# A pooling mixer in front of a gated ConvFFN: zero tile, rows spread by TensorE, whole weights for two tiles, and the second norm turned in transpose mode

## The chip, the cores and the metric

The kernel runs on one core of a Trainium2 chip. The metric is the device time of one execution in microseconds, median of the runs shown. PE is TensorE, DVE VectorE, ACT ScalarE, POOL GpSimd, and SP the queue that issues all transfers of this kernel.

## The reference

One layer on x of 1024 tokens by 1024 columns, float32:

```python
h = rms_norm(x, norm_mix_g)
# pool_mixer: four column groups, causal windows of 2, 4, 8 and 16 tokens
d[g] = window_sum(h[g], w_len) / count - h[g]
y = scale * (einsum('bsgc,gcd->bsgd', d, w) + b)      # w: four 256x256 blocks
x = x + y
f = rms_norm(x, norm_ffn_g)
h = causal_depthwise_conv(f @ w_in, conv_w, conv_b)   # w_in: 1024 x 5632
val, gate = split(h)
out = x + (silu(gate) * val) @ w_out                  # w_out: 2816 x 1024
```

## The kernel before

All products are in float32 accuracy. A large product splits each operand into a high part (float32r, made by a copy on ACT) and the rest (a subtraction on DVE), and adds three products of these. The two ConvFFN products are done in seven block products of halves (a Strassen scheme: P1 to P7), for which sums and differences of blocks are made by DVE. They make up most of the time.

The change is in what comes before: the mixer and the making of the first product's right operand. The tokens lie in eight tiles of 128 (j = 0 to 7). One loop over j, unrolled, has these steps, each some rounds behind the one before:

- `stat(j)` calls `rstd_of` (L127): ACT squares the tile with a row sum, takes a root, and DVE gets the reciprocal and makes it more exact by a Newton step, five [128, 1] operations in all.
- `mixer_norm(j)` (L145): DVE multiplies the window matrix `band` by this, per token.
- `mixer_window(j)` (L188): eight f32 matmuls (`windows`, L149) turn the tile and apply windows and norm (`psd`). The first 16 tokens of a tile also need the tile before: `edges` holds this, made at once for all tiles from `x_edge`, the last 16 rows of each tile (`edge_norm`, `mixer_edges`). Then ACT and DVE split psd into `dh` and `dl`.
- `mixer_weights` and `mixer_bias` (L175, L157), once: DVE scales the mixer's weights by both gains, ACT and DVE split them into `wph` and `wpl`; the bias comes from rows read 128 times over.
- `mixer_out(j)` (L206): 24 matmuls of 256 columns and two of 512 for the bias (`psy`), the residual add on DVE (L217), a store of x1, the second norm's statistic, and DVE scales an identity by it (`diag`).
- `ffn_operand(j)` (L233): eight f32 matmuls with `diag` as the moving operand turn x1 and norm it (`pst`). ACT multiplies seven column blocks by the gain, DVE the eighth (`n2f`). Then come the splits of blocks B11 and B21 for tiles 0 to 3, and for tiles 4 to 7 differences of blocks and their splits.

Matmuls are shown in the trace as one record for float32r and bf16, two for float32. An engine works through its instructions in order. The order is set when the program is built, by a planner that takes what is ready by its own estimates of times, earlier code first; `tc.issue_after(ins)` puts the instructions of a block behind `ins` on the same engine. SP issues transfers in order and waits in order. Tiles of one tag share their buffers; a new one waits until the one before in its place is released. `x0`, `x1` and `x7` lie in the tag "hl", where later the split operands lie. `wp_raw` and `rows_b` lie in the tag "raw", into which `load_in` later loads blocks of w_in.

## Time and profile before

| | |
|---|---|
| median of 3 runs | 721.17 us (720.72 to 721.32) |
| profiled execution, its own time | 723.45 us |
| span of its profile | 721.7 us |
| TensorE busy, instructions | 698.9 us (97%), x3252 |
| VectorE busy | 609.7 us (84%), x941 |
| ScalarE busy | 352.3 us (49%), x566 |
| GpSimd busy | 7.7 us (1%), x33 |
| DMA | 83.83 MB, mean 116 GB/s |

The profile is of one execution. Its span is a little shorter than that execution's time, which also holds what lies before the first and behind the last instruction. Busy times of matmuls overlap, since matmuls are pipelined: the spacing of their starts, which the chain of work gives, is what one costs in a row of them. The same holds for VectorE and ScalarE, where an instruction can start some 0.07 us before the one ahead of it ends.

### The profile page before, as it was taken

To read this page: it belongs to the slowest core of one execution; us is meant where nothing else is said; L and a number is where in the kernel's file an instruction comes from. 1 tells how busy PE (TensorE), PEld (TensorE's weight loads), DVE (VectorE), ACT (ScalarE), POOL (GpSimd) and SP (SyncE) were. 2 spreads that over 40 slices of the span, in tenths; PEclk is the share of its full clock that TensorE was granted. 3 is DMA by queue.
4 is the path that set the end of the run, shared out by engine and by line. 5 is a ranking of instruction groups with operands and counts; after the bars stand their busy time and mean duration, and the time that the engine had idled before them with its cause. 6 is when DMAs were issued, how large, how long until landed. Compare 5 with 4: busy or idle time off the path is not lost.

```text
span 721.7 us, 8803 instructions
## 1 busy us (share of the span) xinstructions
PE 698.9 (97%) x3252; PEld 580.2 (80%) x3252; DVE 609.7 (84%) x941; ACT 352.3 (49%) x566; POOL 7.7 (1%) x33
## 2 busy tenths in 40 slices
...
DMA packets 30881, 83.83 MB, mean 116 GB/s; under 512 B 3335, under 2 KB 4487, under 8 KB 28023
## 3 DMA queue, kind: packets, MB, share of 16 engines
...
## 4 chain that ended last, share of the span: by engine, by line
PE 80%; DVE 11%; DMA 6%; issue 1%; SPq 1%; ACT 1%; DVEq 0%; ACTq 0%
PE Y L303 23%; PE oP L576 21%; PE X L303 15%; PE Z L303 15%; PE psy L214 3%; DMA blk<-g_dram 3%; PE psd L151 2%; DMA x<-in_x_dram 1%; PE pst L237 1%; DVE n2f L271 1%; DVE oBP L70 1%; DVE T L260 1%; DMA blk<-in_w_out_dram 1%; DVE blk L271 1%; DVE oAP L70 1%
## 5 line engine op out<-in xcount | busy, mean ns | idle before, releaser
L576 PE MATMUL oP<-oBP,oAP 128*128 128x512 f32 x924 | 210.8, 390 | 1.0 <-ACT oBP L69 0.6
L576 PEld LDWEIGHTS oP<-oBP,oAP 128*128 128x128 f32 x924 | 173.2, 188 | 38.5 <-DVE oBP L70 1.4
L303 PE MATMUL X<-B,A11s 128*128 128x512 f32 x264 | 65.6, 394 | 0.7 <-DVE A11s L70 0.7
L303 PE MATMUL Y<-T,S2s 128*128 128x512 f32 x264 | 65.1, 394 | 1.1 <-DVE T L260 1.0
L303 PE MATMUL Z<-B,S4s 128*128 128x512 f32 x264 | 64.1, 392 | 0.6 <-DVE r L337 0.6
L303 PE MATMUL Z<-T,S1s 128*128 128x512 f32 x264 | 64.6, 393 | 0.0
L303 PE MATMUL Y<-T,S3s 128*128 128x512 f32 x264 | 64.3, 392 | 0.0
L303 PE MATMUL Y<-T,A22s 128*128 128x512 f32 x264 | 64.1, 392 | 0.0
L303 PE MATMUL X<-B,A12s 128*128 128x512 f32 x264 | 63.4, 390 | 0.0
L303 PEld LDWEIGHTS Y<-T,S2s 128*128 128x128 f32 x264 | 49.2, 188 | 13.2 <-DVE T L260 1.5
L303 PEld LDWEIGHTS X<-B,A11s 128*128 128x128 f32 x264 | 49.3, 188 | 12.3 <-DVE A11s L70 1.1
L303 PEld LDWEIGHTS Z<-B,S4s 128*128 128x128 f32 x264 | 49.5, 188 | 11.8 <-issue 1.1
L303 PEld LDWEIGHTS Z<-T,S1s 128*128 128x128 f32 x264 | 49.5, 188 | 11.4 <-ACT S1s L69 0.2
L303 PEld LDWEIGHTS Y<-T,S3s 128*128 128x128 f32 x264 | 49.6, 188 | 11.2
L303 PEld LDWEIGHTS Y<-T,A22s 128*128 128x128 f32 x264 | 49.5, 188 | 11.1 <-ACT val L350 0.3
L303 PEld LDWEIGHTS X<-B,A12s 128*128 128x128 f32 x264 | 49.5, 188 | 10.3
L361 ACT ACTIVATE gate<-gate 128x1024 f32<-128x1024 f32 x22 | 23.4, 1061 | 43.5 <-DVE gate L352 43.5
L69 ACT ACTIVATE oBP<-blk 128x512 fp32r<-128x512 f32 x32 | 20.2, 633 | 46.9 <-PE oP L576 41.6
L351 DVE SCALAR_TENSOR_TENSOR val<-ha,par_sb,val 128x1023 f32<-128x1023 f32 x22 | 28.2, 1282 | 12.5 <-ACT val L350 12.5
L343 DVE TENSOR_TENSOR ha<-Z,q 128x512 f32<-128x512 f32 x20 | 13.8, 691 | 23.9 <-PE Z L303 23.9
L69 ACT ACTIVATE S4s<-win 128x512 fp32r<-128x512 f32 x22 | 13.9, 633 | 40.4 <-PE Z L303 35.9
L350 ACT ACTIVATE gate<-hb,par_sb 128x1024 f32<-128x1024 f32 x22 | 27.4, 1245 | 11.9 <-DVE hb L345 11.9
(130 smaller groups left out, 1094.2 us busy)
## 6 DMA issues: line engine op xcount, KB each, us to landing
...
g_dram<-val SPq DMA_DIRECT2D x22, 512.0 KB, 2.6
...
x<-in_x_dram SPq DMA_DIRECT2D x8, 512.0 KB, 10.4
x_dram<-x SPq DMA_DIRECT2D x8, 512.0 KB, 2.6
```

The lines of the kernel that those rows point to most:

```text
L69: nc.scalar.activation(t[:, 0, :], src, AF.Copy)
L70: nc.vector.tensor_tensor(t[:, 1, :], src, t[:, 0, :].bitcast(F32), ALU.subtract)
L151: nc.tensor.matmul(ps[:, c * P : (c + 1) * P], src[:, c * P : (c + 1) * P], weights[:, c // 2, :], start=True, stop=True)
L214: nc.tensor.matmul(o, a[:, c, :], w[:, c, :], start=c % 4 == 0 and i == 0, stop=False, skip_group_check=True)
L237: nc.tensor.matmul(ps[:, c * P : (c + 1) * P], x1[:, c * P : (c + 1) * P], diag, start=True, stop=True)
L271: nc.vector.tensor_tensor(out, a, b, ALU.subtract)
L303: nc.tensor.matmul(bank, a[:, i, ks], b[:, l, k, :], start=opens and m == 0, stop=m == 11, skip_group_check=not opens)
L343: tt(hid[n, "a"][:, NH:], bank, hid[n, "q2"], ALU.add)
L350: nc.scalar.activation(t, src, AF.Identity, bias=par_sb[:, CB + f : CB + f + 1], scale=w[2])
L351: nc.vector.scalar_tensor_tensor(t[:, 1:], src[:, : S - 1], w[1], t[:, 1:], op0=ALU.mult, op1=ALU.add)
L361: nc.scalar.activation(gate, gate, AF.Silu)
L576: nc.tensor.matmul(obanks[set_, i], a[:, u, i * P : (i + 1) * P], b[:, v, :], start=opens and g == 0 and m == 0, stop=g == NP2 - 1 and m = ...
```

## The change

- The first transfers are the scale row (on one partition) and both rows as 8 x 128 blocks, then x0, the constants (the first tile's windows now in bf16), the parameters and the weights, x1, x_edge, two rows of the bias, and x2 to x7. The broadcast reads of scale and bias are gone.
- TensorE starts with eight matmuls on a tile of zeros, and runs six more behind the first windows (`keep_warm`). Two matmuls with ones spread the scale row over the partitions, into PSUM, where `mixer_weights` reads it.
- The bias is multiplied and split on 8 partitions and goes by DMA into two rows of a tile that GpSimd has zeroed.
- The norm has three small operations in place of five: the scale by the number of columns is folded into constants (`FOLD`), and root and reciprocal are multiplied in by the instruction that uses them.
- Tiles 0 and 1 are not split: eight f32 matmuls of 256 columns with `wp_raw` take the place of 24. The split of the weights is a step of its own behind the edges' norm.
- The second norm is applied by DVE before the turn: `ffn_norm` multiplies x1 by the statistic and by the gain, which `gain_rows` has spread over the partitions. `ffn_operand` then turns it by `nc.tensor.transpose`, and the splits read PSUM; `n2f` is filled by one ACT copy (half of one for tiles 4 to 7).
- The input sums of the first two hidden blocks are made in rounds 9 and 10 of the loop (`sums_in`).

The diff, cut:

```diff
+FOLD = 2 * D**0.5
...
 NOPS_A = 3
-ACT_GAIN = 7
+XBUFS = 4
+WHOLE = 2
...
     def load_x(j):
-        if j < 2 or j == NS - 1:
+        if j < 2 or j >= 2 + XBUFS:
             xs[j] = work.tile([P, D], F32, tag="hl", name=f"x{j}", bufs=7)
         else:
-            xs[j] = pp.tile([P, D], F32, tag="x", name=f"x{j}", bufs=5)
+            xs[j] = pp.tile([P, D], F32, tag="x", name=f"x{j}", bufs=XBUFS)
...
     wp_raw = raw_tile("wp_raw").rearrange("p a (c d) -> p (a c) d", d=GRP)
-    rows_b = raw_tile("rows_b")
-    scale_b, bias_b = rows_b[:, 0, :], rows_b[:, 1, :]
+    rows_raw = raw_tile("rows_raw")
+    row_sb = rows_raw[:1, 0, :]
+    rows8, bias8 = (rows_raw[:NK, 1, i * NH : i * NH + 2 * P].rearrange("k (r p) -> k r p", p=P) for i in range(2))
+    bias8 = bias8.bitcast(F32R)
+    idle = work.tile([P, NH], BF16, tag="sum", name="idle", bufs=3)
+    nc.vector.memset(idle, 0.0)
+    idle_ps = bank2("idle_ps")[:, :NH]
+    def keep_warm(n):
+        for _ in range(n):
+            nc.tensor.matmul(idle_ps, idle[:, :P], idle, start=True, stop=True)
+    keep_warm(8)
+    nc.sync.dma_start(row_sb, rows[:1, :])
+    nc.sync.dma_start(rows8, rows.rearrange("r (k p) -> k r p", p=P))
     load_x(0)
     nc.sync.dma_start(cst, consts)
-    nc.sync.dma_start(x_edge[HALO:, :], x.rearrange("(j r) d -> j r d", r=P)[: NS - 1, P - HALO :, :])
     nc.sync.dma_start(par_sb, par)
-    nc.sync.dma_start(scale_b, rows[:1, :].to_broadcast([P, D]))
-    load_x(1)
     for g in range(0, NG, 2):
         nc.sync.dma_start(wp_raw[:, 2 * g : 2 * g + 4, :], pool_w[g : g + 2].rearrange("g (k p) d -> p (g k) d", p=P))
-    load_x(2)
-    nc.sync.dma_start(bias_b, rows[1:, :].to_broadcast([P, D]))
-    for j in range(3, NS):
+    b8 = rows8[:, 1, :]
+    nc.vector.tensor_tensor(b8, b8, rows8[:, 0, :], ALU.mult)
+    nc.scalar.activation(bias8[:, 0, :], b8, AF.Copy)
+    nc.vector.tensor_tensor(bias8[:, 1, :], b8, bias8[:, 0, :].bitcast(F32), ALU.subtract)
+    load_x(1)
+    nc.sync.dma_start(x_edge[HALO:, :], x.rearrange("(j r) d -> j r d", r=P)[: NS - 1, P - HALO :, :])
+    spread = work.tile([P, NK, P], F32, tag="hl", name="spread", bufs=7)
+    bias_hl = work.tile([P, D], F32R, tag="hl", name="bias_hl", bufs=7)
+    nc.gpsimd.memset(bias_hl.bitcast(F32), 0.0)
+    for l in range(2):
+        nc.sync.dma_start(bias_hl[l : l + 1, :].bitcast(F32), bias8[:, l, :].bitcast(F32))
+    for j in range(2, NS):
         load_x(j)
     eps_t = const.tile([P, 1], F32, tag="eps", name="eps_t")
-    nc.vector.memset(eps_t, EPS)
+    nc.vector.memset(eps_t, D * EPS)
+    warm = pp.tile([P, 1], F32, tag="warm", name="warm")
+    nc.scalar.activation(warm, eps_t, AF.Sqrt)
     ident = cst[:, :FAC]
     fac = cst[:, FAC:B0].rearrange("p (c t) -> p c t", t=HALO)
-    band0 = cst[:, B0:].rearrange("p (g s) -> p g s", s=P)
+    band0 = cst[:, B0:].bitcast(BF16).rearrange("p (g s) -> p g s", s=P)
...
         nc.scalar.activation(junk, src, AF.Square, accum_out=st[:, 0:1])
...
+        marks[name] = nc.scalar.activation(st[:, 1:2], st[:, 0:1], AF.Sqrt, bias=eps_t).ins
+        nc.vector.tensor_scalar(st[:, 0:1], st[:, 0:1], D * EPS, None, op0=ALU.add)
+        nc.vector.scalar_tensor_tensor(st[:, 3:4], st[:, 1:2], st[:, 1:2], st[:, 0:1], op0=ALU.mult, op1=ALU.add)
+        nc.vector.reciprocal(st[:, 2:3], st[:, 3:4])
+        return st[:, 1:2], st[:, 2:3]
+    def normed(out, src, r):
+        return nc.vector.tensor_scalar(out, src, r[0], r[1], op0=ALU.mult, op1=ALU.mult).ins
+    bands, stats = {}, {}
     def edge_norm():
-        nc.vector.tensor_scalar(edge_band, edge_band, rstd_of(x_edge, "e"), None, op0=ALU.mult)
+        marks["edge"] = normed(edge_band, edge_band, rstd_of(x_edge, "e"))
     def mixer_norm(j):
         t = bands[j] = pp.tile([P, NG, P], F32, tag="bandr", name=f"bandr{j}", bufs=2)
-        nc.vector.tensor_scalar(t, band if j else band0, stats[j], None, op0=ALU.mult)
+        marks[f"band{j}"] = normed(t, band if j else band0, stats[j])
...
+    ones = pp.tile([P, P], F32R, tag="ones", name="ones")
+    nc.vector.memset(ones.bitcast(F32), 1.0)
+    scale_b = []
+    for h in range(2):
+        t = ps_x.tile([P, NH], F32, tag="X", name=f"scale{h}")
+        nc.tensor.matmul(t, ones[:1, :].bitcast(F32), row_sb[:, h * NH : (h + 1) * NH], start=True, stop=True)
+        scale_b += [t[:, :GRP], t[:, GRP:]]
...
     def mixer_weights():
         for c in range(2 * NG):
-            g = c // 2
             nc.vector.scalar_tensor_tensor(
-                wp_raw[:, c, :], scale_b[:, g * GRP : (g + 1) * GRP], par_sb[:, GM + c : GM + c + 1], wp_raw[:, c, :], op0=ALU.mult, op1=ALU.mult
+                wp_raw[:, c, :], scale_b[c // 2], par_sb[:, GM + c : GM + c + 1], wp_raw[:, c, :], op0=ALU.mult, op1=ALU.mult
             )
...
-    ds = {}
+    def split_weights():
+        for c in range(0, 2 * NG, 2):
+            cs = slice(c, c + 2)
+            nc.scalar.activation(wph[:, cs, :], wp_raw[:, cs, :], AF.Copy)
+            nc.vector.tensor_tensor(wpl[:, cs, :], wp_raw[:, cs, :], wph[:, cs, :].bitcast(F32), ALU.subtract)
+    def gain_rows():
+        gain = par_sb[:, GF : GF + NK].unsqueeze(2).to_broadcast([P, NK, P])
+        nc.vector.tensor_tensor(spread, ident[:, None, :].to_broadcast([P, NK, P]), gain, ALU.mult)
+        ps = bank2("ps_gain")
+        flat = spread.rearrange("p k s -> p (k s)")
+        for h in range(2):
+            cols = slice(h * NH, (h + 1) * NH)
+            nc.tensor.matmul(ps[:, cols], ones.bitcast(F32), flat[:, cols], start=True, stop=True)
+        gain_b = work.tile([P, D], F32, tag="ha", name="gain_b", bufs=1)
+        nc.scalar.activation(gain_b, ps, AF.Copy, scale=FOLD)
+        return gain_b
+    ds, gains = {}, []
     def mixer_window(j):
         ps = bank2(f"psd{j}")
-        windows(ps, xs[j], bands.pop(j))
+        last = windows(ps, xs[j], bands.pop(j))
+        if j == 0:
+            with tc.issue_after(last):
+                keep_warm(6)
+        if j == 1:
+            mixer_edges()
         dh = pp.tile([P, NK, P], F32R, tag="dh", name=f"dh{j}", bufs=2)
-        dl = pp.tile([P, NK, P], F32R, tag="dl", name=f"dl{j}", bufs=1)
         ps3 = ps.rearrange("p (c s) -> p c s", c=NK)
         first = ps3[:, :, :HALO]
         if j == 0:
-            nc.vector.tensor_tensor(first, first, fac, ALU.mult)
+            marks["first"] = nc.vector.tensor_tensor(first, first, fac, ALU.mult).ins
         else:
             nc.vector.tensor_tensor(first, first, edges[:, :, j * HALO : (j + 1) * HALO], ALU.add)
+        if j < WHOLE:
+            dh = dh.bitcast(F32)
+            marks[f"whole{j}"] = nc.scalar.activation(dh, ps3, AF.Copy).ins
+            ds[j] = [(dh, wp_raw)]
+            return
+        dl = pp.tile([P, NK, P], F32R, tag="dl", name=f"dl{j}", bufs=1)
         nc.scalar.activation(dh, ps3, AF.Copy)
         nc.vector.tensor_tensor(dl, ps3, dh.bitcast(F32), ALU.subtract)
-        ds[j] = (dh, dl)
+        ds[j] = [(dh, wph), (dh, wpl), (dl, wph)]
...
-        dh, dl = ds.pop(j)
+        terms = ds.pop(j)
         ps = bank2(f"psy{j}")
+        for c in range(NK):
+            o = ps[:, c // 2 * GRP : (c // 2 + 1) * GRP]
+            for i, (a, w) in enumerate(terms):
+                nc.tensor.matmul(o, a[:, c, :], w[:, c, :], start=c % 4 == 0 and i == 0, stop=False, skip_group_check=True)
         for h in range(2):
             cols = slice(h * NH, (h + 1) * NH)
-            for c in range(4 * h, 4 * h + 4):
-                o = ps[:, c // 2 * GRP : (c // 2 + 1) * GRP]
-                for i, (a, w) in enumerate(((dh, wph), (dh, wpl), (dl, wph))):
-                    nc.tensor.matmul(o, a[:, c, :], w[:, c, :], start=c % 4 == 0 and i == 0, stop=False, skip_group_check=True)
-            nc.tensor.matmul(ps[:, cols], mean_w, bias_hl[:, cols], start=False, stop=True, skip_group_check=True)
+            nc.tensor.matmul(ps[:, cols], ones, bias_hl[:, cols], start=False, stop=True, skip_group_check=True)
         x1 = xs.pop(j)
         marks[j] = nc.vector.tensor_tensor(x1, ps, x1, ALU.add).ins
         nc.sync.dma_start(x1_dram[j * P : (j + 1) * P, :], x1)
-        r = rstd_of(x1, f"b{j}")
-        diag = pp.tile([P, P], F32, tag="diag", name=f"diag{j}", bufs=2)
-        nc.vector.tensor_scalar(diag, ident, r, None, op0=ALU.mult)
-        n2s[j] = (x1, diag)
+        n2s[j] = (x1, rstd_of(x1, f"b{j}"))
+    def ffn_norm(j):
+        x1, r = n2s[j]
+        n2 = n2s[j] = pp.tile([P, D], F32, tag="n2", name=f"n2_{j}", bufs=2)
+        nc.vector.tensor_tensor(r[1], r[0], r[1], ALU.mult)
+        nc.vector.scalar_tensor_tensor(n2, x1, r[1], gains[0], op0=ALU.mult, op1=ALU.mult)
...
-        x1, diag = n2s.pop(j)
+        n2 = n2s.pop(j)
         ps = bank2(f"pst{j}")
         for c in range(NK):
-            nc.tensor.matmul(ps[:, c * P : (c + 1) * P], x1[:, c * P : (c + 1) * P], diag, start=True, stop=True)
+            nc.tensor.transpose(ps[:, c * P : (c + 1) * P], n2[:, c * P : (c + 1) * P], ident)
         cols = slice(j * P, (j + 1) * P)
         ps3 = ps.rearrange("p (c s) -> p c s", c=NK)
-        gain = par_sb[:, GF : GF + NK]
-        for c in range(ACT_GAIN):
-            nc.scalar.activation(n2f[:, c, cols], ps3[:, c, :], AF.Identity, scale=gain[:, c : c + 1])
-        rest = slice(ACT_GAIN, NK)
-        nc.vector.tensor_tensor(n2f[:, rest, cols], ps3[:, rest, :], gain[:, rest].unsqueeze(2).to_broadcast([P, NK - ACT_GAIN, P]), ALU.mult)
         lo, hi = slice(0, 4), slice(4, 8)
         if j < NS // 2:
-            split_n(nops["B11"], n2f[:, lo, cols], cols)
-            split_n(nops["B21"], n2f[:, hi, cols], cols)
+            split_n(nops["B11"], ps3[:, lo, :], cols)
+            split_n(nops["B21"], ps3[:, hi, :], cols)
+            nc.scalar.activation(n2f[:, :, cols], ps3, AF.Copy)
             return
         cols0 = slice(cols.start - NH, cols.stop - NH)
-        b11, b12, b21, b22 = n2f[:, lo, cols0], n2f[:, lo, cols], n2f[:, hi, cols0], n2f[:, hi, cols]
+        b11, b12, b21, b22 = n2f[:, lo, cols0], ps3[:, lo, :], n2f[:, hi, cols0], n2f[:, hi, cols]
+        nc.scalar.activation(b22, ps3[:, hi, :], AF.Copy)
         sub(b11, b12, b11)
         split_n(nops["T1"], b11, cols0)
-        sub(b12, b22, b12)
+        sub(n2f[:, lo, cols], b22, b12)
         sub(b21, b21, b22)
...
+    def sums_in(n):
+        a11, a12, a21, a22 = (raws[n][:, i, k * NH : (k + 1) * NH] for i in range(2) for k in range(2))
+        s3 = sums[n, "S3"] = tmp(f"S3_{n}")
+        sub(s3, a11, a21)
+        add(a21, a21, a22)
+        sums[n, "S2"] = a11
+        sub(a11, a21, a11)
+        sums[n, "S4"] = a12
+        sub(a12, a12, a11)
...
         if j < NS:
             mixer_norm(j)
         if j == 0:
+            stat(1)
             edge_norm()
-            stat(1)
         if 0 <= j - 1 < NS:
             mixer_window(j - 1)
         if j == 1:
-            mixer_edges()
-            mixer_weights()
-            mixer_bias()
-        if 0 <= j - 2 < NS:
+            with tc.issue_after(marks["first"]):
+                mixer_weights()
+            with tc.issue_after(marks["edge"]):
+                mixer_out(0)
+        if 1 <= j - 2 < NS:
             mixer_out(j - 2)
+            ffn_norm(j - 2)
+        if j == 2:
+            with tc.issue_after(marks["edge"]):
+                gains.append(gain_rows())
+            ffn_norm(0)
+        if j == 2:
+            with tc.issue_after(marks["edge"]), tc.issue_after(marks["e"]):
+                split_weights()
         if 0 <= j - 4 < NS:
             ffn_operand(j - 4)
         if j in (4, 6):
...
         if 5 <= j <= 8:
             with tc.issue_after(marks[j - 2]):
                 prep_event(j - 5)
+        if j in (9, 10):
+            sums_in(j - 9)
         if j in (8, 10, 11):
             event((8, 10, 11).index(j))
```

## Rows read from the trace of the kernel before

**Rows 1.** Busy time by stretch: stretch, its length, each engine's busy us, clock, DMA, GB/s.
```profile
0.00:8.66 8.66, 0.00 (x0) 0.00 (x0) 1.70 (x8) 4.01 (x5) 7.68 (x33) 1.00 0.78 199
8.66:36.20 27.54, 20.74 (x128) 19.43 (x129) 17.12 (x47) 15.39 (x27) 0.00 (x0) 0.88 0.84 296
36.20:75.75 39.55, 39.55 (x320) 38.51 (x320) 33.97 (x103) 32.23 (x82) 0.00 (x0) 1.00 0.20 81
75.75:111.88 36.13, 33.74 (x170) 27.65 (x168) 36.13 (x57) 23.27 (x48) 0.00 (x0) 1.00 0.20 74
111.88:700.00 588.12, 587.05 (x2561) 480.42 (x2562) 509.57 (x712) 273.33 (x398) 0.00 (x0) 1.00 0.32 113
```

**Rows 2.** Timeline of the opening: start, us, engine, line, operation, operands, count [idle before].
```profile
1.25 0.42 SPq L109 DMA_DIRECT2D cst<-in_consts_dram  x1
...
4.21 1.06 ACT L130 ACTIVATE junk_a<-x 128x1024 bf16<-128x1024 f32 x1 [2.13 <-DMA x<-in_x_dram]
...
5.38 1.28 ACT L131 ACT_TABLE_LOAD   x1
...
6.79 1.53 POOL L88 TENSOR_SCALAR_AFFINE_SELECT band<-band 128x128 f32<-128x128 f32 x6
7.00 0.15 DVE L132 TENSOR_SCALAR st_a<-st_a 128x1 f32<-128x1 f32 x1 [5.90 <-ACT st_a L131]
...
8.66 3.40 PE L151 MATMUL psd<-bandr,x 128*128 128x128 f32 x16 [8.66 <-DVE bandr L147]
11.34 4.54 SPq L81 DMA_DIRECT2D x<-in_x_dram  x5
11.40 1.06 ACT L130 ACTIVATE junk_e<-x_edge 128x1024 bf16<-128x1024 f32 x1 [4.44 <-DMA x_edge<-in_x_dram]
```

**Rows 3.** Chain of work, in order of time: start, us, engine and tile, count.
```profile
33.40 1.44 PE psy L214 x12
...
38.28 0.23 PE psy L215
...
40.19 1.78 PE pst L237 x16
```

**Rows 4.** Busy time by stretch, around the first fall of the clock.
```profile
12.00:14.40 2.40, 0.07 (x1) 0.00 (x0) 1.27 (x7) 1.19 (x4) 0.00 (x0) 1.00 1.08 369
14.40:17.80 3.40, 3.35 (x16) 3.05 (x16) 2.41 (x10) 2.64 (x5) 0.00 (x0) 0.58 1.05 392
```

**Rows 5.** Timeline: the second tile's first product and its residual add.
```profile
31.46 0.39 PE L214 MATMUL psy<-wph,dh 128*128 128x256 f32 x1 [0.71 <-DVE dl L200]
...
36.22 1.20 DVE L217 TENSOR_TENSOR x<-psy,x 128x1024 f32<-128x1024 f32 x1
```

**Rows 6.** Busy time of two single microseconds; the last column is GB/s.
```profile
3.00:4.00 1.00, 0.00 (x0) 0.00 (x0) 0.00 (x0) 0.00 (x0) 1.00 (x5) 1.00 0.98 387
...
9.00:10.00 1.00, 1.00 (x6) 1.00 (x6) 0.00 (x0) 0.00 (x0) 0.00 (x0) 1.00 0.99 156
```

**Rows 7.** Groups of instructions up to 112 us: busy us, mean ns | idle before.
```profile
L242 ACT ACTIVATE n2f<-pst,par_sb 128x128 f32<-128x128 f32 x56 | 16.4, 379 | 4.7 <-PE pst L237 4.7
...
L200 DVE TENSOR_TENSOR dl<-psd,dh 128x1024 fp32r<-128x1024 f32 x8 | 9.7, 1218 | 6.5 <-PE psy L214 6.3
...
L178 DVE SCALAR_TENSOR_TENSOR wp_raw<-rows_b,par_sb,wp_raw 128x256 f32<-128x256 f32 x8 | 3.5, 474 | 0.0
...
L221 DVE TENSOR_SCALAR diag<-cst,st_b 128x128 f32<-128x128 f32 x8 | 2.2, 280 | 0.0
...
L90 POOL MEMSET x_edge<- 16x1024 f32 x1 | 0.9, 942 | 0.3 <-POOLq L640 0.3
```

**Rows 8.** The page: its costliest groups, and its DMA issues with us to landing.
```profile
L351 DVE SCALAR_TENSOR_TENSOR val<-ha,par_sb,val 128x1023 f32<-128x1023 f32 x22 | 28.2, 1282 | 12.5 <-ACT val L350 12.5
...
x_dram<-x SPq DMA_DIRECT2D x8, 512.0 KB, 2.6
```

**Rows 9.** Waits of TensorE after 70 us: us in total, times, longest.
```profile
PE Y L303 <- DVE T L260: 1.0, 1, 1.0
```

42 lines of the change are left out of this document (14 added, 28 removed).

## Prediction

> **What bounds the kernel now.** I read the page first, then the busy times by stretch, then the chain of work, then the timeline of the opening. The execution profiled took 723.45 us, 1.75 us more than its span of 721.7; the median shown is 721.17. All sums are made in the span, and the saving is taken off the median. TensorE is busy 698.9 us of the span, so only about 23 us of idle TensorE can go, beside work that can be taken off it.
>
> [rows 1] say where that idle time lies. Up to 36.2 us TensorE does 20.7 us of work, so 15.5 us are idle there. From 36.2 to 75.75 us it is never idle. From 75.75 to 111.88 us it is idle 2.4 us, and VectorE is busy in all 36.13 us: there the chain of work lies on VectorE, which has to make the operands of the first products. From 111.88 to 700 us TensorE is idle 1.1 us in 588. So the change, which touches only the mixer and the operands after it, is worth what it moves the point 111.88. Two questions decide it: how early the mixer runs at full pace, and how much VectorE has to do from there to 111.88.
>
> The opening in detail [rows 2]: the first x, issued at 0.8, is squared at 4.21, a table load of 1.28 us stands between the square and the root, five small VectorE operations run from 7.00 to 8.12, and the first matmul starts at 8.66. It takes 3.40 us, half the speed of the same work later (1.78 us for 16 records [rows 3]). x_edge is waited for until 11.40. After the 2.4 us from 12.0, in which TensorE did 0.07 us of work, the granted clock falls to 1.2 GHz [rows 4]; a second such fall follows at 25.2. The second tile's psy starts at 31.46 and its residual add at 36.22 [rows 5]. I use that add, "x1add(1)", as the mark of the end of the opening.
>
> **The change, part by part.**
>
> *Transfers.* SP gets two small issues ahead of x0, at 0.42 us each by cst's issue [rows 2], so x0 is issued and lands 0.85 us later: 5.05. The two broadcast reads of 512 KB are gone. x_edge goes from third place to behind the weights and x1. The order of landing before is that of issue, and the rate was 387 GB/s at 3 us but 156 at 9 us [rows 6], while x_edge, par and the broadcast were at the head. Which of them is slow the trace does not show. Up to the weights there are now 1.85 MB, x1 makes 2.35, x_edge 2.8 MB. At 387 GB/s throughout from 2.2 us they land at 7.0, 8.3 and 9.4; at 156 from 5.3 us, where 0.75 MB are in, at 12.3, 15.5 and 18.4. I take 9, 10.5 and 13, nearer the fast end, as one of the three slow suspects is gone. The bias rows now cross SBUF by two DMAs that SP issues after GpSimd has zeroed bias_hl. GpSimd's list ends at 8.32 [rows 2] and a memset of 1024 columns took 0.94 [rows 7], so SP stands until 9.3, and x2 to x7 are queued behind it. Before, SP issued the last five between 11.34 and 15.9 [rows 2], so this costs nothing while the queue still holds the weights, x1 and x_edge; if they are through by 9.4, the queue runs empty for about 1 us, and x2, wanted at 14, still lands at about 13.
>
> *ScalarE and the norm.* The Sqrt table is loaded before the square, but behind a copy of the bias that waits for rows8: issue 1.25, some 2.6 us to land (the shortest median [rows 8]), a VectorE multiply and the copy 0.6, then the load 1.28 and a Sqrt 0.3, so ScalarE is free at 5.9. The square of x0 runs 5.9 to 7.1, the root to 7.4, three small operations in place of five 0.6 (of 1.12), the band 0.5: first matmul at 8.5 against 8.66. Nothing is gained there.
>
> *keep_warm.* Eight bf16 matmuls of 512 columns: 0.23 us each at 2.4 GHz by the bias product of 512 columns [rows 3], twice that at 1.2, so 1.8 to 3.7 us from about 1.2 us on, in time when TensorE has nothing else; then the two scale matmuls (4 records of 0.44, 1.8 us, 3.5 cold), done at 8.4 at the latest. They cost nothing. The first windows then take 1.8 in place of 3.40, and the six matmuls behind them (1.4 us) keep the clock up to the next work.
>
> *Weights and the first tiles.* psd0 is done at 10.3, its first columns fixed at 10.6. VectorE scales eight weight pieces at 0.42 apart (0.474 each [rows 7]) until 14.0, for which the weights have to have landed by 10.6. Tiles 0 and 1 are multiplied whole: eight f32 matmuls of 256 columns, at twice the 0.222 of a 128-column one, 3.55 us against 2.88, so 0.67 more on TensorE per tile and one dl of 1.22 less on VectorE [rows 3, 7]. psy0 no longer waits for the four splits and the bias (2.4 us of VectorE for the bias gone): it ends at 15.8 with its bias product (0.46). Then psd1 to 17.6, the edge windows (x_edge 13, square, root, band: 15.8) to 19.4, psd2 to 21.2, the gain rows (4 records of 0.44) to 22.9, psy1 to 26.9. VectorE's own list to this point: 18.8 us before [rows 1]; less 2.4 for the bias, 2.4 for dl, 0.8 for the shorter norms; plus 1.2 for the spread and 1.2 for the first n2: 15.6, nearly all behind 10.6, so it is ready at 26 at the earliest. x1add(1) then starts at 27, against 36.2. Bounds: 25 with the fast transfers; 30 with the slow ones, since edge_norm is put in front of the splits, the spread and x1add(0).
>
> *The mixer from there.* VectorE per tile gains n2, a scalar_tensor_tensor of 1.28 (1.2 apart [rows 8]) and one small product, and loses diag (0.28 [rows 7], 0.2 apart) and the eighth gain column, of the same shape, and two small operations in each norm. From x1add(1) to x1add(7) that is 6 x 1.14 for the adds, 6 x 0.3 norms, 6 x 1.25 n2, 5 x 1.14 dl, 3.8 for bands, first columns and norms of x, 4.8 + 2.4 for operands, 2.4 for A11 and A12: 35 us, where VectorE was busy 34 in 39.55. ScalarE loses 0.8 a tile (seven gains of 0.38 [rows 7], 0.25 apart, become one copy of 1.0). TensorE loses whatever the turn saves: a transpose stands in no row. Its bounds are 0.06 us each (one record at half the 0.111 of these) and 0.222 (as the product now); 0.5 or 1.78 a tile. I take 0.9, one record at the spacing of these. TensorE then needs about 33 us for the six tiles, 40 at the dear end. VectorE is the longer one and the stretch takes 38.7 with 3.7 us of waits (5.6 before); bounds 36.5 and 41. x1add(7): 65.7 against 75.75.
>
> The Trainium skill ("TensorE: Matmul & The Clock Gate", Part 4) gives about 275 ns for a transpose in a kernel and says that this mode does not bring the full clock. By its price the turn would take 2.2 us a tile, TensorE would set the pace from 27 to the former 111.88 with 76.7 us, and the saving would be 8 us; no run here shows a transpose yet.
>
> *After the mixer.* 36.1 us of VectorE work [rows 1]: plus one n2, less three gain columns and a diag, 36.6. sums_in brings forward the same instructions and adds none. The point 111.88 then lies at 27 + 38.7 + 36.6 = 102.3. TensorE's own work from x1add(1) to there was 73.3 us; even with no saving by the turn it would end at 100.3, so the price of a transpose hardly matters: VectorE covers it.
>
> Sum: 111.88 - 102.3 = 9.6 us; 721.17 - 9.6 = 711.5.
>
> **The rivals.**
>
> *The opening is held by x_edge* (chance 0.2). Everything of VectorE after the weights is ordered behind edge_norm. For it: x_edge took until 11.40 from third place. Against: the slow time is shared by three transfers. At the slow bound x1add(1) is at 30, and waits in the mixer as before make 40 of the 38.7: saving 5.3, so 716.
>
> *VectorE and TensorE both go better* (0.1): fast transfers, 36.5 in the mixer: 25 + 36.5 + 36 = 97.5, saving 14.4, so 707.
>
> *The clock falls, slower* (0.07). VectorE now sets the pace, so TensorE waits some 10 us between 27 and 102. Behind both idle stretches of the opening it fell [rows 4]. If the waits, with the transposes among them, leave the clock at that level, a tile takes 11.2 us (5.6 doubled) in place of 6.4. Three tiles cost 14 and turn the sign; all six cost 29, so 740. Against: the wait of 1.0 us at 102 [rows 9] left the clock full [rows 1], and 10 us over ten tiles make waits of that size. The Trainium skill ("TensorE: Matmul & The Clock Gate", Part 4) would make this likelier, if the transposes count as no work at all.
>
> *Nothing is left of it* (0.05): VectorE waits for ScalarE's copies out of the turned banks. Two copies of 0.66 in each tile come to 1.3, over eight tiles 10.6: the saving is gone, so 721 or 722.
>
> **How the numbers follow.** The forecast has 0.58, with its own range 708.5 to 714.5. Predicted 711.5. The range 706 to 717.5 takes in the bounds of the transfers and of the mixer, and leaves out the last two rivals and the edge of the good one. 0.2% is 1.4 us, about what a measurement can tell: the last two rivals share 0.12 between no change (0.05) and slower (0.07); faster 0.88.
>
> **What would show it.** First psd at about 8.5, of 1.8 us; no stretch at 1.2 GHz after 5 us; psy0 ending near 16; x1add(1) near 27; n2 1.25 us each; VectorE over 90% busy from 27 to 100 with TensorE waiting in gaps under 1.5 us. Wrong would make it: a first psd after 10 us, x_edge after 16, a clock below full behind the transposes, or VectorE idle over 6 us between 27 and 66.

## The result, and the profile after

The changed kernel took 725.56 us (median of 4 runs, 723.46 to 725.79) and the kernel before, beside it on the same chip, 720.98 (720.72 to 721.32): a ratio of 1.005, 95% interval 1.0025 to 1.0074. It is slower, by some 4 us, where 711.5 was predicted, in a range of 706 to 717.5. On another chip it took 725.27 against 721.98, a ratio of 1.0043 (1.0027 to 1.006). Its profiled execution took 725.76 us with a span of 724.0.

The busy time by stretch of the changed kernel, in the stretches of [rows 1] (PE, PEld, DVE, ACT, POOL, then the clock, DMA share, GB/s):
```profile
0.00:8.66 8.66, 7.24 (x13) 2.21 (x13) 2.29 (x9) 3.24 (x6) 8.03 (x34) 1.00 0.68 220
8.66:36.20 27.54, 21.57 (x103) 17.29 (x103) 16.36 (x44) 15.61 (x28) 0.85 (x1) 0.88 0.66 210
36.20:75.75 39.55, 35.14 (x269) 32.82 (x268) 35.99 (x72) 25.43 (x46) 0.00 (x0) 1.00 0.25 94
75.75:111.88 36.13, 35.16 (x175) 28.44 (x173) 35.65 (x54) 21.68 (x35) 0.00 (x0) 1.00 0.23 88
```
TensorE's 7.24 us in the first stretch are the zero tile and the rows spread, not the kernel's own products. In the second it does hardly more than before; in the third, where before it was never idle, 4.4 us are now idle while VectorE works.

TensorE's timeline in the opening (start, us, tile, count, and in brackets the idle time ahead with what ended it):
```profile
1.42 3.59 PE L123 MATMUL idle_ps<-idle 128*128 128x512 bf16 x8 [1.42 <-DVE idle L118]
4.94 3.78 PE L191 MATMUL scale<-rows_raw,ones 1*128 1x512 f32 x4
8.65 3.78 PE L182 MATMUL psd<-bandr,x 128*128 128x128 f32 x16
...
21.62 0.61 PE L182 MATMUL ps_edges<-edge_band,x_edge 128*128 128x128 f32 x4
27.84 3.75 PE L224 MATMUL ps_gain<-spread,ones 128*128 128x512 f32 x4 [5.62 <-DVE st_a L162]
31.39 2.81 PE L182 MATMUL psd<-bandr,x 128*128 128x128 f32 x16
34.04 3.62 PE L265 MATMUL psy<-wp_raw,dh 128*128 128x256 f32 x16
```
Here the opening went wrong. After the edges TensorE stands for 5.62 us, and what it stands for is ps_gain, the rows of the second gain, which nothing needs yet; psd2 and psy1, which the mixer does need, are queued behind it. What ps_gain waits for is its operand `spread`, on VectorE (done at 27.70; the bracket names the instruction that ended last before the start), and what that waits for is on ScalarE:
```profile
26.15 0.15 DVE L162 TENSOR_SCALAR st_b<-st_b 128x1 f32<-128x1 f32 x1 [1.65 <-ACT st_b L161]
26.34 0.22 DVE L164 SCALAR_TENSOR_TENSOR st_b<-st_b 128x1 f32<-128x1 f32 x1
26.48 1.22 DVE L219 TENSOR_TENSOR spread<-cst,par_sb 128x1024 f32<-128x1024 f32 x1
```
```profile
16.93 1.06 ACT L160 ACTIVATE junk_e<-x_edge 128x1024 bf16<-128x1024 f32 x1 [1.74 <-DMA x_edge<-in_x_dram]
...
23.88 1.06 ACT L160 ACTIVATE junk_b<-x 128x1024 bf16<-128x1024 f32 x1 [0.59 <-DVE x L270]
...
24.93 1.01 ACT L248 ACTIVATE dh<-psd 128x1024 f32<-128x1024 f32 x1
25.84 0.28 ACT L161 ACTIVATE st_b<-st_b,eps_t 128x1 f32<-128x1 f32 x1
```
The spread has needed nothing but cst and par, which VectorE had read many microseconds earlier; it runs at 26.48 only because it is queued behind the norm of x1 of tile 0, whose Square and root ScalarE made at 23.88 and 25.84. dh1, the operand of psy1, is done at 25.94. So psy1 starts 8.1 us after its operand. The granted clock fell within the idle stretch: it is 0.64 and 0.68 in the two windows below, and 0.50, the level of 1.2 GHz, from 26.5 to 33.0, so ps_gain and the first part of psd2 run at half rate (3.75 and 2.81 us):
```profile
25.00:30.00 5.00, 2.15 (x3) 1.15 (x4) 3.15 (x12) 3.79 (x9) 0.00 (x0) 0.64 0.84 292
30.00:35.00 5.00, 5.00 (x23) 3.86 (x23) 2.04 (x4) 1.97 (x3) 0.00 (x0) 0.68 0.00 0
```
x1add(1) starts at 38.16 (36.22 before), x1add(7) at 79.99 (75.75), and the first store of a gated row, a mark behind the mixer, at 128.91. Before it was at 127.91. A second profile of the kernel before, an execution of 720.72 us, has neither of the two falls of the clock of [rows 1, 4] and its first store is 2.2 us earlier. SP's timeline of after, then of that second profile of before, and the second stretch of the latter:
```profile
128.91 0.33 SPq L426 DMA_DIRECT2D g_dram<-val  x1
```
```profile
125.71 0.33 SPq L363 DMA_DIRECT2D g_dram<-val  x1
```
```profile
8.66:36.20 27.54, 20.48 (x146) 19.18 (x147) 19.32 (x57) 17.66 (x31) 0.00 (x0) 1.00 0.82 299
```
Against that second profile, 3.2 us of the loss lie ahead of the first store; in the second profile of after (run 7) they are 4.5. Between the first store and the nineteenth all four profiles take 328.8 us. From the nineteenth of the 22 stores to the last output it took 256.7 and 256.1 us in two profiles of after, 255.7 and 255.2 in two of before. The stretch up to the 22nd store is 58.37 us in all four, so this second part of the loss, 0.4 to 1.5 us, lies in the product of the output.

### The profile page after: what moved, and what is told of

It reads as the page before. It is cut to its first block, busy times and chain, and to the rows that moved or that the text cites. A ratio compares the mean times of both kernels' runs of the same rounds, so it can differ in the third digit from the quotient of the medians.

```text
span 724.0 us, 8607 instructions
## 1 busy us (share of the span) xinstructions
PE 704.9 (97%) x3194; PEld 575.2 (79%) x3194; DVE 612.1 (85%) x907; ACT 344.2 (48%) x519; POOL 8.9 (1%) x34
## 4 chain that ended last, share of the span: by engine, by line
PE 76%; DVE 11%; DMA 8%; ACT 2%; issue 1%; SPq 1%; DVEq 0%; ACTq 0%
PE Y L366 23%; PE oP L650 21%; PE X L366 15%; PE Z L366 14%; DMA blk<-g_dram 2%; DMA x_edge<-in_x_dram 2%; PE psy L265 2%; DVE n2f L324 1%; DVE T L313 1%; DVE oBP L76 1%; DVE oAP L76 1%; PE psd L182 1%; DMA blk<-in_w_out_dram 1%; DMA B21s<-in_w_out_dram 1%; DMA win<-in_w_in_dram 1%
## 5 line engine op out<-in xcount | busy, mean ns | idle before, releaser
L366 PEld LDWEIGHTS Y<-T,S2s 128*128 128x128 f32 x264 | 49.3, 188 | 12.5 <-DVE T L313 0.9
L366 PEld LDWEIGHTS Y<-T,S3s 128*128 128x128 f32 x264 | 49.6, 188 | 11.2
L366 PEld LDWEIGHTS X<-B,A12s 128*128 128x128 f32 x264 | 49.4, 188 | 10.2
L414 DVE SCALAR_TENSOR_TENSOR val<-ha,par_sb,val 128x1023 f32<-128x1023 f32 x22 | 28.2, 1282 | 12.5 <-ACT val L413 12.5
L76 DVE TENSOR_TENSOR oBP<-blk,oBP 128x512 fp32r<-128x512 f32 x32 | 22.0, 687 | 11.9 <-ACT oBP L75 11.9
```

The costliest lines, as they stand in the source:

```text
L76: nc.vector.tensor_tensor(t[:, 1, :], src, t[:, 0, :].bitcast(F32), ALU.subtract)
L366: nc.tensor.matmul(bank, a[:, i, ks], b[:, l, k, :], start=opens and m == 0, stop=m == 11, skip_group_check=not opens)
L414: nc.vector.scalar_tensor_tensor(t[:, 1:], src[:, : S - 1], w[1], t[:, 1:], op0=ALU.mult, op1=ALU.add)
```

## The experiments

All are edits of the changed kernel. The ratio is to the kernel before, beside them on the same chip; its median there was 721.82 (runs 1 to 4), 721.98 (5 to 8) and 721.79 (9 to 11). The last four columns are starts in the profile, in us.

| run | median | ratio (95%) | x1add(1) | x1add(7) | first store | fifth store |
|---|---|---|---|---|---|---|
| before, profile of [rows 1 to 9] | | | 36.22 | 75.75 | 127.91 | 186.82 |
| 12 before, second profile | | | 34.03 | 73.56 | 125.71 | 184.64 |
| after | 725.56 | 1.0050 (1.0025 to 1.0074) | 38.16 | 79.99 | 128.91 | 187.81 |
| 7 after again | 725.27 | 1.0043 (1.0027 to 1.0060) | 39.94 | 81.28 | 130.19 | 189.12 |
| 1 spread by GpSimd | 721.45 | 1.0008 (0.9995 to 1.0021) | 34.49 | 75.83 | 124.75 | 183.67 |
| 2 gain rows later | 720.47 | 0.9981 (0.9966 to 0.9995) | 33.15 | 76.51 | 125.40 | 184.33 |
| 3 old norm | 721.56 | 0.9995 (0.9978 to 1.0011) | 33.45 | 74.73 | 122.62 | 183.65 |
| 4 = 1, x_edge third | 721.18 | 0.9997 (0.9984 to 1.0009) | 33.46 | 75.70 | 124.61 | 183.53 |
| 5 = 1, n2 off VectorE (GpSimd) | 726.47 | 1.0066 (1.0051 to 1.0080) | 35.63 | 79.92 | 127.09 | 187.70 |
| 6 old norm, tile elsewhere | 718.71 | 0.9949 (0.9931 to 0.9966) | 32.15 | 73.19 | 121.07 | 181.63 |
| 8 = 1, no zero tile | 721.48 | 0.9988 (0.9974 to 1.0001) | 35.09 | 78.12 | 127.02 | 185.95 |
| 9 = 1, n2 off VectorE (ScalarE) | 719.31 | 0.9964 (0.9948 to 0.9980) | 33.17 | 74.18 | 121.90 | 182.93 |
| 10 = 6, no early sums | 720.84 | 0.9983 (0.9972 to 0.9993) | 33.00 | 73.81 | 125.91 | 184.82 |
| 11 = 6, x_edge third | 717.16 | 0.9944 (0.9926 to 0.9962) | 30.45 | 71.72 | 119.61 | 180.23 |

The first store is not the same place in every kernel. In runs 3, 5, 6 and 11 it stands behind 194 records of the first product on TensorE, in run 9 behind 192, in all others behind 201; at 0.23 us each that shifts the mark by 1.6 to 2.1 us. At the fifth store all have 458. So kernels of the two groups are compared at the fifth. The first product's busy time up to the first store and from there to the fifth, in run 6 and then in run 10:
```profile
0.00:121.07 121.07, 45.56 (x194) 36.13 (x195) 0.96 0.35 120
121.07:181.63 60.56, 60.56 (x265) 49.52 (x265) 1.00 0.29 105
```
```profile
0.00:125.91 125.91, 47.99 (x201) 37.19 (x202) 0.96 0.34 116
125.91:184.82 58.91, 58.91 (x258) 48.15 (x257) 1.00 0.29 107
```

**1 and 2: the gain rows.** In 1 the spread goes to an idle engine, in 2 the gain rows go behind psy1.
```diff
-        nc.vector.tensor_tensor(spread, ident[:, None, :].to_broadcast([P, NK, P]), gain, ALU.mult)
+        nc.gpsimd.tensor_tensor(spread, ident[:, None, :].to_broadcast([P, NK, P]), gain, ALU.mult)
```
```diff
         if 1 <= j - 2 < NS:
             mixer_out(j - 2)
+            if j == 3:
+                gains.append(gain_rows())
+                ffn_norm(0)
             ffn_norm(j - 2)
-        if j == 2:
-            with tc.issue_after(marks["edge"]):
-                gains.append(gain_rows())
-            ffn_norm(0)
```


> The spread of the second gain is made by GpSimd, which is idle from 9.5 us, instead of VectorE; nothing else is edited, and ps_gain keeps its place in TensorE's queue behind the edges and ahead of psd2 and psy1. My theory: the 5.62 us that TensorE waited at 22.2 us, and the half clock behind it (ps_gain 3.75 us, psd2 2.81, in place of some 1.8 each), come from the spread that stood in VectorE's queue behind the second norm of tile 0. Then ps_gain runs at about 22.5, psd2 behind it, psy1 starts at about 27 instead of 34.0, x1add(1) at about 31 instead of 38.2, and the whole falls by 6 to 8 us, to 718 to 720. Rival A: tile 1 is held by x_edge (landed at 16.9) and by the ScalarE and VectorE work behind it, so psy1 cannot start before about 31 to 32: x1add(1) at 35 to 36, whole 722 to 724. Rival B: VectorE's pace through the mixer decides, and the lead is given back by the point where the first operand of the products is ready (112.8): whole within 2 us of the changed kernel.

> The gain rows are traced one round later: ps_gain stands in TensorE's queue behind psy1, and the second norms of tiles 0 and 1 follow it. VectorE still makes the spread. My theory: psd2 and psy1 no longer stand behind a matmul that waits, so psy1 starts at about 26 to 27 (dh1 was there at 25.94) and x1add(1) at 30 to 31; the second norm of tile 0 comes some 4 us later than with the spread made early, which the mixer can take since its transposes come two rounds later. Whole 717 to 720. If this run and the one with GpSimd's spread gain alike, it was the place in the queue and not VectorE's 1.2 us. Rival A (x_edge holds tile 1): x1add(1) at 35 to 36, 722 to 724. Rival B (VectorE's pace decides): within 2 us of the changed kernel.

Measured: TensorE's timeline of run 1 has ps_gain 4.0 us earlier, at its full rate, and psy1 at 27.38.
```profile
23.80 1.95 PE L224 MATMUL ps_gain<-spread,ones 128*128 128x512 f32 x4 [1.21 <-ACT edges L198]
25.59 1.95 PE L182 MATMUL psd<-bandr,x 128*128 128x128 f32 x16
27.38 3.62 PE L265 MATMUL psy<-wp_raw,dh 128*128 128x256 f32 x16
```
One word takes 4.2 us off the first store and 0.35 to 0.42% off the time; moving the place takes 3.5 us off the first store and 0.62 to 0.69% off the time. With either, nothing is left of the loss: the stuck gain rows are its cause. (Run 2 has the later stores and the shorter time, since it takes 255.0 us behind the nineteenth store and run 1 256.2; why is open.) But the times stop at the kernel before or 0.2% below it, 9 to 10 us above the forecast, and x1add(1) is at 33 to 34, not 31: the theory was right on the place and too large on its worth.

**3 and 6: the opening with the old second norm.** The diagonal matrix, ScalarE's seven gains and VectorE's one return; gain rows, spread, n2 and transposes go.
```diff
-        n2 = n2s[j] = pp.tile([P, D], F32, tag="n2", name=f"n2_{j}", bufs=2)
-        nc.vector.tensor_tensor(r[1], r[0], r[1], ALU.mult)
-        nc.vector.scalar_tensor_tensor(n2, x1, r[1], gains[0], op0=ALU.mult, op1=ALU.mult)
+        d = pp.tile([P, P], F32, tag="diag", name=f"diag{j}", bufs=2)
+        normed(d, ident, r)
...
-            nc.tensor.transpose(ps[:, c * P : (c + 1) * P], n2[:, c * P : (c + 1) * P], ident)
+            nc.tensor.matmul(ps[:, c * P : (c + 1) * P], x1[:, c * P : (c + 1) * P], d, start=True, stop=True)
```
Run 6 differs from run 3 in one word, the pool of a tile of 32 bytes per partition:
```diff
-    gain_sb = const.tile([P, NK], F32, tag="gain", name="gain_sb")
+    gain_sb = pp.tile([P, NK], F32, tag="gain", name="gain_sb")
```


> The changed kernel with the second norm of before: the diagonal matrix as moving operand, the gain brought in by ScalarE's seven small copies and VectorE's one; there are no gain rows, no spread, no n2 and no transposes. The opening is that of the changed kernel. My theory: the opening alone is worth what was forecast once nothing stands in TensorE's queue: psy1 at 26 to 27, x1add(1) at 30 to 31 (36.2 before), then before's pace of 75.7 us from there to the first operand at 111.9, so that this point comes at 106 and the whole at 714 to 717. The second norm in transpose mode by itself is then worth what lies between this run and the ones with the gain rows out of the way, by the two paces (75.7 against 74.7) about 1 us. Rival C: ScalarE, freed of nothing here, becomes late in the mixer and the point comes at 109 or later, 719 or more.

> The run with the second norm of before once more, with its 32-byte gain tile in a pool that is closed after the mixer instead of the one that stays, so that nothing behind the mixer lies elsewhere than in the changed kernel. In the earlier run the first g_dram store came 2.1 us sooner than with GpSimd's spread and transposes (122.62 against 124.75), but each of the 17 rounds of products then took 19.44 us instead of 19.28. If the place of the operands makes that difference, the rounds take 19.28 here, the first store comes at 122 to 123, and the whole falls to about 718 to 719, 2 to 3 us below before. If the rounds stay at 19.44, it is something else of the old norm, and the whole stays at about 721.5.

Measured: in run 3 the first store comes 2.1 us earlier than in run 1, and the time is the same. Of the 2.1 us, 1.6 are the shift of the mark; at the fifth store the two are equal, in a profile of run 3 that is of the slowest of its twelve executions (724.11 us, median 721.56). Behind that the rounds are longer. SP's timeline, in run 3 and then in run 6:
```profile
378.04 0.33 SPq L431 DMA_DIRECT2D g_dram<-val  x1
...
397.49 0.33 SPq L431 DMA_DIRECT2D g_dram<-val  x1
```
```profile
374.43 0.33 SPq L431 DMA_DIRECT2D g_dram<-val  x1
...
393.70 0.33 SPq L431 DMA_DIRECT2D g_dram<-val  x1
```
A round of products takes 19.45 us in run 3 and 19.27 in run 6, 14 rounds on average 19.44 and 19.28. The instructions and their order are the same; only where tiles lie in SBUF differs. Run 6 is clearly below both kernels. It is 0.59% below run 1 and 0.32% below run 2: with the opening unblocked, the turned norm, with its gain rows, costs 4.2 us by the one and 2.3 by the other, each uncertain by some 1.6 us, where the prediction gave it nothing to lose.

**4 and 11: x_edge.** Its load goes back to third place, with the transposes (4) and with the old norm (11).
```diff
     nc.sync.dma_start(cst, consts)
+    nc.sync.dma_start(x_edge[HALO:, :], x.rearrange("(j r) d -> j r d", r=P)[: NS - 1, P - HALO :, :])
     nc.sync.dma_start(par_sb, par)
...
-    nc.sync.dma_start(x_edge[HALO:, :], x.rearrange("(j r) d -> j r d", r=P)[: NS - 1, P - HALO :, :])
```


> As the run with GpSimd's spread, and x_edge is loaded in its old place, right behind the constants and ahead of the parameters and the weights, so that it lands near 8 instead of 16.9; weights and x1 come later by its 460 KB, about 1.5 us at the 340 GB/s of the other transfers. Read against the run with GpSimd's spread alone. My theory: x_edge is a second, smaller wait: the band of the edges and psd1's first columns come earlier, x1add(1) 1 to 2 us earlier at most, whole 0 to 2 us less. Rival A: x_edge is what holds tile 1; then x1add(1) falls by 4 us or more and the whole with it. Rival D: the weights, later by 1.5 us or more, hold psy0 and all behind it, and the whole grows by 1 to 2 us.

> As the run of the old norm at its place (718.7), with x_edge loaded in its old place behind the constants. With the transposes this moved x1add(1) by 1.0 us and the first store by only 0.1, since VectorE was the longer engine from there. Here TensorE sets the pace (busy 5.0 of 5 us from 25 to 80), so what the opening gains should stay: x1add(1) 1 us earlier at 31, first store at 120, whole 717.5 to 718. If the weights, now later, hold psy0, nothing or a loss of 1 us.

Measured: x1add(1) 1.0 us earlier in run 4 and 1.7 in run 11. With the transposes the first store gains 0.1, with the old norm 1.5; the times differ by less than their intervals (1.0008 to 0.9997, 0.9949 to 0.9944). So neither theory is shown by the time, and the clock disturbs both comparisons of profiles. Behind the same wait of 2.87 us the same product ran at full rate in run 1 and not in runs 4 and 8, in this order:
```profile
41.39 2.05 PE L182 MATMUL psd<-bandr,x 128*128 128x128 f32 x16 [2.87 <-DVE dl L253]
```
```profile
40.36 3.15 PE L182 MATMUL psd<-bandr,x 128*128 128x128 f32 x16 [2.87 <-DVE dl L253]
```
```profile
41.98 3.78 PE L181 MATMUL psd<-bandr,x 128*128 128x128 f32 x16 [2.87 <-DVE dl L251]
```
The granted clock from 40 to 45 us is 1.00 in run 1, 0.66 in run 4 and 0.63 in run 8. So tile 3 takes 8.31 us in run 4 and 7.43 in run 1, and the lead of run 4 over run 1, 1.0 us at tile 2, is 0.15 us at tile 3: it was lost where the clock fell, and not to VectorE's pace, which the expectation of run 11 names. The other way round, psd2 runs at half rate in run 6 (first line) and not in run 11 (second), which makes up most of the 1.7 us:
```profile
24.55 3.58 PE L182 MATMUL psd<-bandr,x 128*128 128x128 f32 x16 [2.19 <-issue]
```
```profile
24.05 2.02 PE L182 MATMUL psd<-bandr,x 128*128 128x128 f32 x16 [1.18 <-issue]
```

Which transfer is slow, left open in the prediction, is seen in the busy time by window, of after and then of run 4 (last column GB/s):
```profile
5.00:10.00 5.00, 5.00 (x11) 2.45 (x11) 1.08 (x4) 1.44 (x3) 4.51 (x16) 1.00 0.99 339
10.00:15.00 5.00, 5.00 (x23) 3.76 (x23) 2.53 (x7) 2.16 (x4) 0.00 (x0) 1.00 1.05 213
```
```profile
5.00:10.00 5.00, 5.00 (x11) 2.45 (x11) 1.08 (x4) 1.25 (x3) 4.55 (x16) 1.00 0.94 192
10.00:15.00 5.00, 5.00 (x22) 3.69 (x22) 2.52 (x7) 1.02 (x1) 1.90 (x1) 1.00 1.06 376
```
The slow 5 us move with x_edge, at an equal DMA share. x_edge is the slow one, and it delays what stands behind it: in run 4 x1 lands for 15.1, in run 1, ahead of x_edge, for 13.4.

**5 and 9: VectorE's n2.** In 5 GpSimd multiplies by the gain row and ScalarE by the norm; in 9 ScalarE multiplies by the norm, and the gain's multiplication is left out, so that its result is not the reference's; its gain rows are still made. The edit of 5:
```diff
-        nc.vector.scalar_tensor_tensor(n2, x1, r[1], gains[0], op0=ALU.mult, op1=ALU.mult)
+        nc.gpsimd.tensor_tensor(n2, x1, gains[0], ALU.mult)
+        nc.scalar.activation(n2, n2, AF.Copy, scale=r[1])
```


> As the run with GpSimd's spread, and VectorE's n2 (1.28 us a tile, 8 tiles) is taken off it: GpSimd multiplies x1 by the gain row (about 1.9 us by its spread of the same size), ScalarE multiplies the product by the norm (about 1.0 us). Theory V: since the turn, VectorE sets the mixer's pace (7.4 us a tile, VectorE busy 36.1 of 36.1 us from 76 to 112 and TensorE not). Then the tiles come up to 1.28 us sooner each, some 6.2 to 6.6 us, where TensorE (5.6 + 0.9) takes over; x1add(7), at 75.8 there, falls to about 70, the first g_dram store from 124.8 to about 118 to 119, and the whole by 5 to 6 us, to about 716. Rival: the pace is a chain through several engines (TensorE, ScalarE's Square, VectorE's norm, n2, TensorE), and a longer chain by way of GpSimd makes it slower or leaves it: first store at 124 or later, whole 721 or more.

> As the run with GpSimd's spread, but VectorE's n2 (1.28 us, eight times) is left out and ScalarE writes n2 as x1 times the norm (about 1.0 us); the gain's multiplication is left out, so this kernel does not apply the second gain. In the run with GpSimd's product VectorE's operations on two SBUF operands took up to 1772 ns in place of 683 while GpSimd worked, so it could not show what VectorE's relief is worth; here GpSimd stands still. Theory V (VectorE's load sets the mixer's pace since the turn): x1add(1) to x1add(7) falls from 41.3 to 36 to 38 us, the first g_dram store from 124.8 to 117 to 119, the whole to 714 to 717. Rival: the pace is a chain through several engines, which is as long with ScalarE's n2 as with VectorE's; the stretch stays at 40 to 42 us and the whole at 720 to 722.

Measured in 5: slower than run 1 by 0.58%. GpSimd's timeline, and VectorE's beside it:
```profile
43.05 2.40 POOL L278 TENSOR_TENSOR n<-x,gain_b 128x1024 f32<-128x1024 f32 x1 [3.74 <-DVE st_a L164]
```
```profile
44.04 1.69 DVE L169 TENSOR_SCALAR bandr<-band,st_a 128x512 f32<-128x512 f32 x1
45.66 0.68 DVE L328 TENSOR_TENSOR win<-win 128x512 f32<-128x512 f32 x1
```
The band, 0.54 us elsewhere, takes 1.69: it lasts until GpSimd is done. One of the two subtractions for A11s took 2.86 us instead of 0.68. The seven operations that were so held lost 10.0 us together, and the eight n2 had been 10.2. What VectorE was spared it lost again, so the run says nothing on its pace. The Trainium skill ("SBUF — State Buffer", "SBUF: two separate sides") says that VectorE and GpSimd share a port pair that one instruction holds to its end; these rows agree.

Measured in 9: 0.9964, 0.44% or 3.2 us below run 1, between what theory V and its rival had said, and the first store at 121.9, not 117 to 119. The busy time from 34 to 76 us, of runs 1, 9 and 6:
```profile
34.00:76.00 42.00, 36.10 (x277) 33.75 (x278) 38.96 (x80) 28.15 (x52) 0.00 (x0) 1.00 0.22 88
```
```profile
34.00:76.00 42.00, 37.97 (x282) 35.39 (x281) 33.91 (x77) 35.72 (x61) 0.00 (x0) 0.96 0.20 81
```
```profile
34.00:76.00 42.00, 41.83 (x340) 40.59 (x339) 37.12 (x83) 34.36 (x88) 0.00 (x0) 1.00 0.29 109
```
Relieved of n2, VectorE is idle 8 us and TensorE still 4; x1add(1) to x1add(7) takes 41.0 as against 41.3, as the rival had it. Three tiles come at 6.1 to 6.3 us, the others at 7.0 to 8.3, with waits between the engines and a granted clock of 0.50 from 41 to 44 us. Of the 2.9 us at the first store 2.1 are the shift of the mark; the fifth comes 0.7 us earlier than in run 1. So the time shows that VectorE's relief is worth about half of what theory V asked for, but the profile does not show it in the mixer's pace; there neither engine is full, and waits between them and the clock hold the tiles. How these share it was not separated.

**8 and 10: two parts taken out.** Run 8 drops keep_warm(8) and keep_warm(6) from run 1; run 10 drops the two sums_in from run 6.
```diff
-        if j in (9, 10):
-            sums_in(j - 9)
```


> As the run with GpSimd's spread, without the fourteen matmuls on the zero tile. My theory: in the changed kernel's profile eight of them from 1.4 us and the two scale matmuls behind them left TensorE at half its rate until about 12 us (psd0 3.78 us), so they bring nothing, and the scale matmuls behind them (to 8.7) even hold psd0 by 1 us: whole within 1 us of the run with them, psd0 started at 7.7 and of 3.4 to 3.8 us. Rival (the zero tile does its work, by bringing the full clock by 12 us): psd1, the edges and psy0 run at half rate too, psy0 in about 7 us in place of 3.7, x1add(0) at 25 or later instead of 23.0, whole 2 to 4 us longer.

> As the run of the old norm at its place (the changed opening, 718.7), and the two calls that make the input sums of the first two products inside the mixer are taken out, so that these sums are made where they were before. There, x1add(7) came at 73.2 (75.8 before) but the first store 47.9 us behind it (52.2 before). Theory: the 4.3 us come from the sums, which fill VectorE's free time while TensorE sets the mixer's pace; without them the first store comes 51 to 52 us behind x1add(7), and the whole is 721.5 to 723. Rival: the tail is shorter for another reason (operands of the mixer ready sooner), the sums only move, and the whole stays within 1 us.

Measured in 8: the same time (0.9988 against 1.0008, the intervals overlap). The timeline of TensorE in run 8:
```profile
2.54 3.75 PE L190 MATMUL scale<-rows_raw,ones 1*128 1x512 f32 x4 [2.54 <-DMA rows_raw<-in_rows_dram]
7.73 3.39 PE L181 MATMUL psd<-bandr,x 128*128 128x128 f32 x16 [1.44 <-DVE bandr L168]
```
psd0 takes 3.39 us, against 3.78 with the zero tile in after and 2.51 in the profile of run 1. psy0 did not fall back to half rate either (14 records in 3.29 us). The profile's later stores, 2.3 us behind those of run 1, are 0.6 us at x1add(1) and 1.7 in the tile in which the clock fell, as shown above; run 1 does not have that fall. In 10: from x1add(7) to the first store 52.1 us, as before (52.2), against 47.9 with the sums; 1.6 of these 4.2 us are the shift of the mark. To the fifth store it is 111.0 against 108.4: the sums are worth 2.6 us there, and 2.5 us (0.34%) of the time.

**7 and 12: the two kernels again.**

> The changed kernel once more, for the spread of its runs on the chip on which the experiments run and for a second profile. Its first four runs had a median of 725.56. Expected: 725 to 726, x1add(1) at 37 to 39, first g_dram store at 128 to 130. If the loss varies with the granted clock of the opening, the profile's opening differs and the times spread by 2 to 4 us.

> The kernel before once more, for a second profile. Its profiled execution took 723.45 against a median of 721 to 722, and x1add(1) came at 36.2, the first g_dram store at 127.9. If the difference lies in the opening, where TensorE twice fell to half its clock, a faster execution shows x1add(1) and the first store 1 to 3 us earlier at a mean clock nearer 1; if it lies in the product of the output, the first store stays and the stretch from the last store of the gated rows to the last output store (255.7 us) is shorter.

Measured: after stays at 725 and shows the 5.62 us wait ahead of ps_gain a second time. Before: x1add(1) at 34.03 and the clock at 1.00 throughout, so the opening's clock is worth 2.2 us between two executions. The stretch behind the nineteenth store is 0.5 us shorter; it is the 255.7 us of the expectation, where "the last store of the gated rows" is the nineteenth of 22.

## Why the prediction was wrong

By the ratios, in parts of 721.8 us: the opening alone with the old norm and without early sums (run 10) gains 1.2 us; the early sums gain 2.5 more (run 6); the turned norm costs 4.2 (run 1); the stuck gain rows cost 2.5 to 3.0 (after). That is a loss of 3.1 to 3.6. By way of run 2 the norm costs 2.3 and the stuck rows 4.5 to 5.0; how the two share their 7 us is not sharper than that. The prediction had 9.2 of gain for the opening and 0.4 for the rest.

The step that failed is **Weights and the first tiles**, with x1add(1) at 27. It is 38.16, and that is 11.2 of the 14.1 us by which the time missed. Four things were missed:
- The gain rows were entered as 1.8 us of TensorE's work between psd2 and psy1. What they wait for was not asked. In the queue they stand ahead of psd2, and their spread stands on VectorE behind a norm that comes from x1add(0). Worth 3.7 us at x1add(1) (run 1), 5.0 when moved (run 2). The step had this wait at nothing.
- Without them it is still 32 to 34.5. In run 1 the other 7.5 us lie in three places. The edges' windows end at 22.6, where the sum had 19.4: x_edge is there at 17.3, and its Square, norm and band follow. Behind them TensorE stands 1.21 us until ScalarE has copied the edges, a wait that the sum had at nothing; psy1 is through at 31.46, for 26.9. And x1add(1) starts 3.0 us later still, for 0.1, since VectorE's queue has the band and dl of later tiles and two early sums ahead of it:
```profile
31.57 0.54 DVE L169 TENSOR_SCALAR bandr<-band,st_a 128x512 f32<-128x512 f32 x1
32.02 0.68 DVE L324 TENSOR_TENSOR S<-win 128x512 f32<-128x512 f32 x1
32.75 1.23 DVE L253 TENSOR_TENSOR dl<-psd,dh 128x1024 fp32r<-128x1024 f32 x1
33.89 0.68 DVE L327 TENSOR_TENSOR win<-win 128x512 f32<-128x512 f32 x1
34.49 1.22 DVE L270 TENSOR_TENSOR x<-psy,x 128x1024 f32<-128x1024 f32 x1
```
  In run 6 psy1 stands behind psd2, which starts at 24.55 and takes 3.58 us, at a granted clock of 0.50 from 25 to 28. The step counted TensorE's list and VectorE's sum, and not the waits of one queue for another.
- x_edge landed at 16.9, not 13, within the bounds given. That was the first rival (0.2). Loaded third, it brought x1add(1) only 1.0 us (run 4), as the weights and x1 came later, and the rival's time of 716 missed even without the stuck gain rows (721.45 and 720.47).
- The mark of before, 36.22, held 2.2 us of one execution's low clock, and the saving was taken off a median that has less of it.

*Transfers*: the weights landed at 9.7 (9 predicted), and the products needed no wait for them; SP stood until 9.5 (9.3). x1 landed at 13.4 in run 1 (10.5), x_edge at 16.9 (13). x2 was issued at 5.49, ahead of the bias rows and not behind them. *ScalarE and the norm*: the first matmul came at 8.65 for 8.5, but by luck: the band was ready at 7.72, and the zero tile and the scale matmuls held TensorE until 8.7. *keep_warm*: so it was not free at that place (psd0 starts at 7.73 without it, in run 8), but the time does not show it. It brought nothing: the eight matmuls took 3.59 us, near the upper bound of 3.7, the four records 3.78, over theirs of 3.5, and psd0 stayed at half rate (3.78 for 1.8 us).

*The mixer from there*: 41.8 us for 38.7, over the bound of 41. The transposes were 0.9 us a tile as estimated. TensorE's timeline and group:
```profile
43.09 1.03 PE L293 MATMUL pst<-cst,n 128*128 128x128 f32 x8
...
45.54 2.05 PE L182 MATMUL psd<-bandr,x 128*128 128x128 f32 x16 [1.41 <-DVE dl L253]
```
```profile
L293 PE MATMUL pst<-cst,n 128*128 128x128 f32 x42 | 5.6, 272 | 0.0
```
One takes 272 ns, but eight take 1.03 us, 0.11 from one to the next. The Trainium skill's 275 ns ("TensorE: Matmul & The Clock Gate", Part 4) agrees with the first number; summed eight times it would have been 2.2 us. TensorE was faster by the turn, and it did not matter: VectorE got n2 (1.28 us) and the early sums, and TensorE waits for dl 1.2 to 1.4 us in three of the tiles. The step did not count the sums: six of the eight, 4.1 us of VectorE, run between x1add(1) and x1add(7). *After the mixer*: from x1add(7) to the first store 48.9 us, against 52.2 before; 36.6 had been given for a part that was 36.1. One step was too short by 3.1 and the other too long by 3.7, and both together were right to a microsecond. The sums that moved from the second to the first fit that, but no run of the turned norm without them tells; with the old norm (runs 6 and 10) they made the mixer only 0.2 us longer.

The rival of the falling clock had the sign, but in after not the mechanism: waits of 1.2 to 1.4 us between tiles left the clock at 1.00, and it fell only in the 5.62 us of the stuck matmul. In its relatives it was nearer: in runs 4, 5, 8 and 9 the clock went to 1.2 GHz once inside the mixer, for 3 to 7 us, next to waits of 2.1 to 2.9 us, and in run 1 the same 2.87 us left it full. ScalarE's copies out of the turned banks held TensorE 0.7 us in all, so the last rival did not come.

What stays open: the 0.4 to 1.5 us behind the nineteenth store. That stretch took 254.5 to 256.9 us over all profiles, with no order that follows the edits.
